# RWKV operands in one layout for both directions, elementwise steps on all 128 partitions of DVE, token shift read from the accumulators, Gram products in two halves of 64 columns

## The chip, the cores and the metric

The kernel runs on one core of a Trainium2 chip. The metric is the device time of one execution in microseconds, taken as the median of the runs. A core has a matrix engine (PE in the profile, with its weight loads apart as PEld), three engines for elementwise work (DVE, ACT and POOL), and SP, which here only issues DMAs. Each engine runs its own queue in order; semaphores tie the queues together.

## The reference

One block of a hybrid model: 512 latent tokens and 256 context tokens of width 1024 are normalised, modulated and projected by one wide matrix; three mixers (an RWKV-7 recurrence in both directions, a convolution of 31 taps, an mLSTM) work on the projections, are gated, merged and added to the input; an MLP follows. The change touches the RWKV features and their recurrence:

```python
def _token_shift(u, mu_prev, mu_next):
    prev = jnp.pad(u, ((0, 0), (1, 0), (0, 0)))[:, :-1]
    nxt = jnp.pad(u, ((0, 0), (0, 1), (0, 0)))[:, 1:]
    return u + mu_prev * (prev - u) + mu_next * (nxt - u)
...
    for d, (wd, ad) in enumerate(((wd_f, ad_f), (wd_b, ad_b))):
        w_log = -jax.nn.softplus(-(w0[d] + jnp.tanh(wd) @ w2[d]).astype(jnp.float32)) - 0.5
        decay = jnp.exp(-jnp.exp(w_log))
        a = jax.nn.sigmoid((a0[d] + ad @ a2[d]).astype(jnp.float32))
        k_d = k.astype(jnp.float32) * (1.0 + (a - 1.0) * k_a)
...
    def step(S, inp):
        w_t, k_t, v_t, kk_t, a_t = inp[:5]
        S = (S * w_t[:, :, None, :]
             - jnp.einsum('bhvk,bhk->bhv', S, kk_t)[..., None] * (kk_t * a_t)[:, :, None, :]
             + v_t[..., None] * k_t[:, :, None, :])
        y = jnp.einsum('bhvk,bhk->bhv', S, inp[5]) if emit else None
```

There are 8 heads of 64 channels, handled as 4 pairs. The recurrence runs over the context first and then over the latent tokens, forwards and backwards.

## The kernel before

Channels lie on partitions and tokens along the free axis. The matrices are fp32; a weight block of 128x512 is split into a rounded part (`whi`, cast on ACT, L152) and a remainder (`wlo`, subtracted on POOL, L153), and every product is three matmuls per block of 128 rows: x high by w high, x low by w high, x high by w low. `dense` (L250 and after) does this for one block of 128 outputs, into accumulators `dl` (512 latent tokens) and `dc` (256 context tokens) that share three PSUM buffers. It takes two such splits per call.

A scheduler that simulates the program puts the instructions of each engine in order; inside an engine that order is then fixed, so an instruction that waits holds up all that stand behind it on its engine. The program passes these stages, by the time of the trace: the norm and first modulation (0 to 54 us); the convolution's input and its first 62 taps (L291, on DVE), beside the shifted low-rank inputs and the keys (54 to 150); the receptances, the operands of the eight heads, the values and the rest of the convolution's input (150 to 322); the mLSTM with the other taps and the first pair's Gram products (322 to 597); the weaves (597 to 862), in which the chain of one pair, the gates' products and the next pair's preparation are interleaved; the last weave (862 to 1000); the merge and the MLP (1000 to 1430).

The *token shift* (`shifted`, L302) copies the accumulators to a padded tile `U` on ACT (L307, L311) and forms the three terms on DVE: `Ut` = om times `U` (L314), plus mu_p times `U` one token earlier (L315), plus mu_n times `U` one token later (L323).

The *operands* of head h (`operands`, L338) are made for both directions at once, forwards on partitions 0 to 63, backwards on 64 to 127. `BK` holds for each of 12 chunks of 64 tokens the normalised key kk and the key k, loaded from `kb` in the order kk, k on the first half and k, kk on the second. `ct` is the running sum of the log decay over a chunk (scans L365, L366, one for each direction on its half), `E` its Exp (L367, with a column of ones at each end of a chunk) and `en` the Exp of the opposite sign. `al` is kk times the shifted `E` (POOL, L379 and L380, on each half) and r times `E` (DVE, L382). `BK` is multiplied by `en` (POOL, four times L386), by 1 + the tanh of the learning rate on kk (DVE, L389, on each half) and by another function of it on k (DVE, L393, on each half). The results are spilled (`sp_al`, `sp_bk`) and loaded later.

The *Gram products* (`gram`, L973 and after) take, per head, direction and chunk, the 64 rows of that direction of `BK` as 128 stationary columns (both kinds) and of `AL` as streamed columns, 128 for a latent chunk and 64 for a context one (L989); DVE multiplies the results by the masks gmf and gmb into `LT`, `LR` and the other half of `AL` (L991 to L996). The *chain* (L1098) makes one step for both directions: `ch` = AL by SV (L1113), times the inverse `LT` (L1119), copied as U to `UV` (ACT, L1122), then the update of the state (L1128, L1129).

A table of the names in the rows: cy, cz, z and dwh belong to the taps; kb, BK, E, ct, cw, al, rd, PL to the operands; pg, AL, BK to the Gram products; dg (L531) are the gates' products.

## Time and profile before

| what | us |
| --- | --- |
| runs: 1431.49, 1431.73, 1427.99; median | 1431.49 |
| span of the profiled execution | 1429.6 |
| PE busy | 1271.3 (89%) |
| DVE busy | 903.0 (63%) |
| POOL busy | 689.4 (48%) |
| ACT busy | 496.4 (35%) |
| PE busy in 150 to 322 us | 128.4 of 172 |
| POOL busy in 150 to 322 us | 150.2 of 172 |
| DVE busy in 150 to 322 us | 146.9 of 172 |

Only the span is known of the profiled execution's own time; the median of the runs lies 1.9 us above it. A share of busy time over the whole span is a mean over stages with different limits, so the stages are read apart. An idle stretch has behind it, after an arrow, what ended it. Matmuls overlap, so that the busy time of a run of matmuls is less than the sum of their lengths; a logical fp32 product of the small kind is two passes in the trace.

### The profile page before, as it was taken

The numbers are of one execution on the slowest core, as the hardware profiler recorded it, in microseconds if no ns is written. First come the engines' busy times: TensorE is split into PE (matmuls) and PEld (weight loads), VectorE is DVE, ScalarE is ACT, GpSimd is POOL, SyncE is SP. The second block draws the span as 40 slices with busy tenths as digits, with TensorE's granted clock in tenths as the row PEclk, the third lists the DMA queues.
The fourth block names the chain that finished last, engine by engine and source line by source line (L and its number), as shares of the span: only waits on it lengthen the run. The fifth ranks groups of instructions, "written<-read, shape, count | busy, mean of one in ns | idle before, by whom it ended". The sixth has DMA issues, their size and how long they took to land.

```text
span 1429.6 us, 21049 instructions
## 1 busy us (share of the span) xinstructions
PE 1271.3 (89%) x7620; PEld 985.8 (69%) x7620; DVE 903.0 (63%) x1518; ACT 496.4 (35%) x1024; POOL 689.4 (48%) x651
## 2 busy tenths in 40 slices
PE   6989986857698989789989998888999999999997
PEld 1578765635587877566757665566778888888886
DVE  2689888988736699379598895868657543300202
ACT  3422534423222222134244344532354344422322
POOL 0463499990854544233243344533455454444442
PEclk9999998887899998899699998999999999999999
DMA  9211466554162232433244134587544433343332
GB/s 363 67 60 58 119 182 205 171 182 147 39 185 72 93 107 67 128 101 100 72 135 117 45 97 156 185 258 231 205 153 146 134 111 96 111 144 99 125 96 88
DMA packets 113359, 187.81 MB, mean 131 GB/s; under 512 B 23124, under 2 KB 41812, under 8 KB 112232
## 3 DMA queue, kind: packets, MB, share of 16 engines
q1 hardware_dynamic: 113256, 186.47, 41.6%
q8 instruction: 60, 0.98, 0.3%
q14 instruction: 43, 0.35, 0.1%
HBM read 148.64 MB, written 29.40 MB: 125 GB/s over the span
## 4 chain that ended last, share of the span: by engine, by line
PE 58%; DVE 21%; DMA 7%; POOL 7%; issue 5%; ACT 2%; SPq 1%; DVEq 0%; POOLq 0%; ACTq 0%
PE pt L1281 15%; PE pd L1350 12%; PE dl L262 8%; PE dg L531 5%; POOL wlo L153 4%; PE pg L989 3%; DMA wad<-wada 3%; DVE N L1032 3%; PE pr L215 2%; DVE tmp L1030 2%; PE dc L262 2%; DVE cy L291 2%; POOL BK L386 1%; PE ch L1113 1%; DVE N L1025 1%
## 5 line engine op out<-in xcount | busy, mean ns | idle before, releaser
L153 POOL TENSOR_TENSOR wlo<-raw,whi 128x512 fp32r<-128x512 f32 x296 | 440.3, 1493 | 492.9 <-ACT whi L152 437.6
L152 ACT CAST whi<-raw 128x512 fp32r<-128x512 f32 x296 | 181.8, 618 | 358.1 <-PE pt L1281 113.8
L262 PE MATMUL dl<-hh,wlo 128*128 128x512 f32 (+1 forms) x368 | 153.6, 418 | 24.8 <-POOL wlo L153 24.7
L262 PE MATMUL dl<-hh,whi 128*128 128x512 f32 (+1 forms) x368 | 154.5, 420 | 0.7 <-DVE lf L716 0.7
L262 PE MATMUL dl<-hl,whi 128*128 128x512 f32 (+1 forms) x368 | 152.6, 415 | 0.0
L1376 DVE TENSOR_TENSOR x<-pt,modb 128x512 f32<-128x512 f32 x8 | 5.5, 689 | 154.7 <-PE pt L1281 154.7
L1350 PE MATMUL pd<-h2l,whi 128*128 128x512 f32 (+1 forms) x272 | 102.6, 379 | 0.7 <-POOL h2l L1333 0.7
L262 PEld LDWEIGHTS dl<-hh,wlo 128*128 128x128 f32 (+1 forms) x368 | 73.6, 200 | 42.1 <-POOL wlo L153 26.6
L1350 PE MATMUL pd<-h2h,wlo 128*128 128x512 f32 (+1 forms) x272 | 102.0, 377 | 0.0
L1350 PE MATMUL pd<-h2h,whi 128*128 128x512 f32 (+1 forms) x272 | 101.1, 378 | 0.2 <-ACT h2h L1330 0.2
L1281 PE MATMUL pt<-whi,h1l 128*128 128x512 f32 x256 | 99.6, 389 | 0.0
L1281 PE MATMUL pt<-whi,h1h 128*128 128x512 f32 x256 | 99.6, 389 | 0.0
L1281 PE MATMUL pt<-wlo,h1h 128*128 128x512 f32 x256 | 99.1, 389 | 0.0
L262 PEld LDWEIGHTS dl<-hh,whi 128*128 128x128 f32 (+1 forms) x368 | 73.8, 200 | 17.0 <-DVE lf L716 2.1
L262 PEld LDWEIGHTS dl<-hl,whi 128*128 128x128 f32 (+1 forms) x368 | 73.6, 200 | 15.0 <-issue 0.5
L1126 POOL TENSOR_TENSOR sps<-SV,PL 64x128 f32<-64x128 f32 x88 | 40.1, 455 | 79.0 <-DVE SV L1129 75.5
L1354 DVE TENSOR_TENSOR relu<-relu 128x512 f32<-128x512 f32 x32 | 39.5, 1238 | 56.0 <-ACT relu L1353 55.9
L627 DVE SCALAR_TENSOR_TENSOR accm<-wad,sc,accm 128x512 f32<-128x512 f32 x56 | 56.7, 1013 | 27.0 <-DMA wad<-wada 26.6
L531 PE MATMUL dg<-hh,whi 128*128 128x512 f32 x144 | 66.5, 462 | 0.0
L531 PE MATMUL dg<-hl,whi 128*128 128x512 f32 x144 | 66.4, 461 | 0.0
L531 PE MATMUL dg<-hh,wlo 128*128 128x512 f32 x144 | 65.6, 456 | 0.0
L989 PE MATMUL pg<-AL,BK 64*128 64x128 f32 (+1 forms) x384 | 59.1, 311 | 5.5 <-DVE AL L996 4.5
(388 smaller groups left out, 2942.0 us busy)
## 6 DMA issues: line engine op xcount, KB each, us to landing
raw<-wblk SPq DMA_DIRECT2D x296, 256.0 KB, 2.8
wad<-wada SPq DMA_DIRECT2D x64, 256.0 KB, 3.8
wada<-wada SPq DMA_DIRECT2D x8, 1024.0 KB, 17.5
sp_bk<-BK SPq DMA_DIRECT2D x8, 768.0 KB, 3.5
BK<-sp_bk SPq DMA_DIRECT2D x8, 768.0 KB, 4.5
sp_g<-gt SPq DMA_DIRECT2D x24, 256.0 KB, 2.1
sp_al<-al SPq DMA_DIRECT2D x8, 640.0 KB, 3.2
AL<-sp_al SPq DMA_DIRECT2D x16, 256.0 KB, 5.8
```

The costliest lines, as they stand in the source:

```text
L152: A.copy(hi[:, :], raw[:, :])
L153: G.tensor_tensor(lo[:, :], raw[:, :], hi[:, :], ALU.subtract)
L215: PE.matmul(pr[:, :], lhsT=sc[:, k, :], rhs=wa[q * 2 + k // 4][:, k % 4, :], start=(k == 0), stop=(k == KT - 1))
L262: PE.matmul(ps_[0:M, :], lhsT=w[:, ko:ko + M], rhs=x[seg][:, k, :], start=(n == 0), stop=(n == 3 * KT - 1))
L531: yield lambda w=w, x=x, k=k, ko=ko, n=n: PE.matmul(ps[:, :], lhsT=w[:, ko:ko + P], rhs=x[:, k, :], start=(n == 0), stop=(n == 3 * KT - 1))
L627: V.scalar_tensor_tensor(o, t[:, :], sc[:, k, 0:1], o, ALU.mult, ALU.add)
L989: PE.matmul(ps[:, i, :, :], lhsT=BK[dd, c, :, :], rhs=AL[d][dd, b0:b0 + w, :], start=True, stop=True)
L1032: V.tensor_tensor(N[:, s + 1:32, 0:s], N[:, s + 1:32, 0:s], tv, ALU.add)
L1126: last["Pool"] = G.tensor_tensor(sps[hf], SV[d][hf, c, :, :], PL[hf, c, :].unsqueeze(2).to_broadcast([64, 2, CH]), ALU.mult)
L1281: PE.matmul(pss[i][:, :], lhsT=x[:, k, ts_], rhs=w[:, :], start=(k == 0 and n == 0), stop=(k == nk - 1 and n == 2))
L1350: PE.matmul(ps[:, ts_], lhsT=w[:, ko:ko + P], rhs=x[:, k, ts_], start=(k == 0 and n == 0), stop=(k == 7 and n == 2))
L1354: V.tensor_tensor(t[:, :], t[:, :], t[:, :], ALU.mult)
```

## The change

Five things, all on the RWKV path.

1. Token shift: `U` and `Ut` go. ACT writes om times the accumulator into the destination; two scalar_tensor_tensor of DVE per accumulator add the neighbours, read from PSUM at an offset of one (511 and 255 elements).
2. Operands: `BK` is loaded in the same order on both halves. `E` has no padding; a second tile `Ep` holds the shifted Exp, made by two more Exps on ACT, each on 64 partitions. The two products of `al` and the product of `BK` with `en` are one DVE operation each on 128 partitions, as are the two steps with the learning rate. POOL keeps the small copies to `PL`.
3. Keys: the shifted k goes to a tile of the "vj" tag; ACT writes it into `kb`, plain and scaled (before, DVE wrote both).
4. Gram products: 64 stationary columns at a time, kk's into the direction's own half of the PSUM partitions and k's into the other, so twice as many matmuls; `al` holds r first and then kk, and the masks' blocks are exchanged.
5. Chain: U of both directions lies on partitions 0 to 63, V on 64 to 127.

```diff
     def shifted(b, ctx, name, bufs=1, dst=None):
-        U = S1.tile([P, 771], F32, tag="U", name="U", bufs=2)
-        ps = dense(B_RW + b, True, ctx)
...
-        V.tensor_scalar(tmp[:, 0:n], U[:, 1:1 + n], om[:, b:b + 1], None, ALU.mult)
-        V.scalar_tensor_tensor(tmp[:, 0:n], U[:, 0:n], C("mu_p", b), tmp[:, 0:n], ALU.mult, ALU.add)
...
+        for ps, a, z in zip(pss, (0, NT), (NT, T)):
+            n = z - a
+            A.activation(dst[:, a:z], ps[:, :], AF.Copy, scale=om[:, b:b + 1])
+            V.scalar_tensor_tensor(dst[:, a + 1:z], ps[:, 0:n - 1], C("mu_p", b), dst[:, a + 1:z], ALU.mult, ALU.add)
+            V.scalar_tensor_tensor(dst[:, a:z - 1], ps[:, 1:n], C("mu_n", b), dst[:, a:z - 1], ALU.mult, ALU.add)
...
-        SY.dma_start(BK[HF[0]], kb[HF[h]])
-        for x in range(2):
-            SY.dma_start(BK[HF[1], :, x, :], kb[HF[h], :, 1 - x, :])
...
+            SY.dma_start(BK[HF[d]], kb[HF[h]])
...
-        A.activation(E[:, :, 1:CH + 1], ct.rearrange("p (c t) -> p c t", c=NCH), AF.Exp, scale=-0.5 * RALPHA)
+        A.activation(E[:, :], ctf, AF.Exp, scale=-0.5 * RALPHA)
+        A.activation(Ep[0:64, :, 1:CH], ct[0:64, :, 0:CH - 1], AF.Exp, scale=-0.5 * RALPHA)
+        A.activation(Ep[64:128, :, 0:CH - 1], ct[64:128, :, 1:CH], AF.Exp, scale=-0.5 * RALPHA)
...
-            G.tensor_tensor(ALl[:, :, 0, :], kk3[:, 0:8, :], E[dd, 0:8, o:o + CH], ALU.mult)
-            G.tensor_tensor(al[dd, 16:20, :], kk3[:, 8:12, :], E[dd, 8:12, o:o + CH], ALU.mult)
...
+        V.tensor_tensor(al[:, 8 * CH:20 * CH].rearrange("p (c t) -> p c t", t=CH), BK[:, :, 0, :], Ep[:, :, :], ALU.mult)
+        V.tensor_tensor(al[:, 0:8 * CH], rj[:, :], E[:, 0:NT], ALU.mult)
...
-                G.tensor_tensor(BK[:, c, x, :], en3[:, c, :], BK[:, c, x, :], ALU.mult)
...
-            V.scalar_tensor_tensor(BK[dd, :, d, :], ta3[dd], 1.0, BK[dd, :, d, :], ALU.add, ALU.mult)
...
+        V.tensor_tensor(BK[:, :, :, :], BK[:, :, :, :], en3.unsqueeze(2).to_broadcast([P, NCH, 2, CH]), ALU.mult)
+        V.scalar_tensor_tensor(BK[:, :, 0, :], ta3, 1.0, BK[:, :, 0, :], ALU.add, ALU.mult)
...
+        V.tensor_tensor(BK[:, :, 1, :], ta3, BK[:, :, 1, :], ALU.mult)
...
+        kj = shifted(4 + j, True, "vj", 2).rearrange("p (c t) -> p c t", t=CH)
+        A.copy(kb[:, :, 1, :], kj)
+        A.activation(kb[:, :, 0, :], kj, AF.Copy, scale=C("kk", j))
...
-                    PE.matmul(ps[:, i, :, :], lhsT=BK[dd, c, :, :], rhs=AL[d][dd, b0:b0 + w, :], start=True, stop=True)
...
+                    for x, hf in ((0, dd), (1, od)):
+                        PE.matmul(ps[hf, i, :, :], lhsT=BK[dd, c, x, :], rhs=al[:, c] if lat else AL[d][dd, 8 + c:9 + c, :],
+                                  start=True, stop=True)
...
-                    last["PE"] = PE.matmul(ch[hf, 1, h, :], lhsT=TT[hf, h * 12 + c, :], rhs=xs[hf, h, :], start=True, stop=True)
+                    last["PE"] = PE.matmul(ch[HF[0], 1, h, :], lhsT=TT[hf, h * 12 + c, :], rhs=xs[hf, h, :], start=True, stop=True)
...
-                last["ACT"] = A.copy(UV[d][hf, c, :, :], ch[hf, 1])
+                last["ACT"] = A.copy(UV[d][HF[0], c, :, :], ch[HF[0], 1])
```

The scheduler then writes another order. On DVE, at the first token shift among the taps, before:

```order
L291 SCALAR_TENSOR_TENSOR cy_564<-z_563,dwh,cy_564 128x512
L291 SCALAR_TENSOR_TENSOR cy_483<-z_482,dwh,cy_483 128x512
L291 SCALAR_TENSOR_TENSOR cy_564<-z_563,dwh,cy_564 128x512
L291 SCALAR_TENSOR_TENSOR cy_483<-z_482,dwh,cy_483 128x512
L291 SCALAR_TENSOR_TENSOR cy_564<-z_563,dwh,cy_564 128x512
L314 TENSOR_SCALAR Ut<-U,dv 128x769
L291 SCALAR_TENSOR_TENSOR cy_483<-z_482,dwh,cy_483 128x512
L291 SCALAR_TENSOR_TENSOR cy_564<-z_563,dwh,cy_564 128x512
L315 SCALAR_TENSOR_TENSOR Ut<-U,par,Ut 128x769
```

and the same place now, from the same tap on (the lines of the changed kernel have other numbers: the taps are still L291, L310 and L311 are the two neighbours of the token shift, `dl` and `dc` the accumulators):

```order
L291 SCALAR_TENSOR_TENSOR cy_564<-z_563,dwh,cy_564 128x512
L310 SCALAR_TENSOR_TENSOR vj<-dl,par,vj 128x511
L291 SCALAR_TENSOR_TENSOR cy_483<-z_482,dwh,cy_483 128x512
L291 SCALAR_TENSOR_TENSOR cy_564<-z_563,dwh,cy_564 128x512
L311 SCALAR_TENSOR_TENSOR vj<-dl,par,vj 128x511
L291 SCALAR_TENSOR_TENSOR cy_483<-z_482,dwh,cy_483 128x512
L310 SCALAR_TENSOR_TENSOR vj<-dc,par,vj 128x255
L291 SCALAR_TENSOR_TENSOR cy_564<-z_563,dwh,cy_564 128x512
```

The first operation of the token shift moved four taps forward, and it is one that reads an accumulator.

On DVE, in the middle of the operands, one head before (with pieces of its neighbours, which is how the order mixes them):

```order
L365 SCALAR_TENSOR_TENSOR ct<-scm,cw 64x768
L366 SCALAR_TENSOR_TENSOR ct<-scm,cw 64x768
L389 SCALAR_TENSOR_TENSOR BK<-ct,BK 64x12x64
L382 TENSOR_TENSOR al<-rd,E_715 128x8x64
L389 SCALAR_TENSOR_TENSOR BK<-ct,BK 64x12x64
L281 SCALAR_TENSOR_TENSOR U<-tg,dl 128x8x64
L393 TENSOR_TENSOR BK<-ct,BK 64x12x64 x2
L365 SCALAR_TENSOR_TENSOR ct<-scm,cw 64x768
```

and one head now (L352 and L353 are the scans, L366 and L367 the products of `al`, L370 the product with `en`, L371 and L373 the steps with the learning rate):

```order
L352 SCALAR_TENSOR_TENSOR ct<-scm,cw 64x768
L353 SCALAR_TENSOR_TENSOR ct<-scm,cw 64x768
L367 TENSOR_TENSOR al<-rd,E_716 128x512
L366 TENSOR_TENSOR al<-BK,Ep_717 128x768
L370 TENSOR_TENSOR BK<-BK,cw 128x1536
L371 SCALAR_TENSOR_TENSOR BK<-ct,BK 128x12x64
L281 SCALAR_TENSOR_TENSOR U<-tg,dl 128x8x64
L373 TENSOR_TENSOR BK<-ct,BK 128x12x64
L352 SCALAR_TENSOR_TENSOR ct<-scm,cw 64x768
```

What POOL did between has come to DVE, and the next head's scans stand behind the last product of this one. On POOL, the same place before:

```order
L153 TENSOR_TENSOR wlo<-raw,whi 128x512
L386 TENSOR_TENSOR BK<-cw,BK 128x6x64 x2
L379 TENSOR_TENSOR al<-BK,E_715 64x8x64
L380 TENSOR_TENSOR al<-BK,E_715 64x256
L279 MEMSET U 128x8x15
L280 MEMSET U 128x8x15
L386 TENSOR_TENSOR BK<-cw,BK 128x6x64 x2
L379 TENSOR_TENSOR al<-BK,E_715 64x8x64
L380 TENSOR_TENSOR al<-BK,E_715 64x256
L153 TENSOR_TENSOR wlo<-raw,whi 128x512
```

and now (L363 are the copies to `PL`):

```order
L363 COPY PL<-E_714 64x12 x2
L153 TENSOR_TENSOR wlo<-raw,whi 128x512 x9
L363 COPY PL<-E_716 64x12 x2
L153 TENSOR_TENSOR wlo<-raw,whi 128x512 x7
L363 COPY PL<-E_714 64x12 x2
```

Between two heads' copies only the splits of the weights are left on POOL.

## Rows read from the trace of the kernel before

**Rows 1.** Stages: start:end, length, busy us (x instructions) per engine, PEclk, DMA share, GB/s
```profile
54.00:150.00 96.00, 90.03 (x469) 76.42 (x467) 79.69 (x101) 27.20 (x52) 52.52 (x63) 0.95 0.23 69
150.00:322.00 172.00, 128.36 (x567) 97.66 (x566) 146.86 (x118) 70.88 (x117) 150.15 (x133) 0.88 0.60 175
...
597.00:862.00 265.00, 247.68 (x2426) 178.73 (x2427) 207.12 (x404) 100.58 (x283) 92.37 (x127) 0.91 0.34 100
```

**Rows 2.** Groups, 150 to 322 us: xcount | busy us, mean ns | idle before, releasers
```profile
L386 POOL TENSOR_TENSOR BK<-cw,BK 128x384 f32<-128x384 f32 x32 | 52.7, 1660 | 0.5
L153 POOL TENSOR_TENSOR wlo<-raw,whi 128x512 fp32r<-128x512 f32 x27 | 46.5, 1728 | 7.3 <-ACT whi L152 6.4 <-PE dl L262 0.6
...
L389 DVE SCALAR_TENSOR_TENSOR BK<-ct,BK 64x768 f32<-64x768 f32 x16 | 30.0, 1874 | 13.3 <-POOL BK L386 13.1
L379 POOL TENSOR_TENSOR al<-BK,E 64x512 f32<-64x512 f32 x16 | 26.2, 1635 | 4.3 <-DMA BK<-kb 3.5
L393 DVE TENSOR_TENSOR BK<-ct,BK 64x768 f32<-64x768 f32 x16 | 24.6, 1540 | 4.0 <-ACT ct L390 3.7
L366 DVE TENSOR_TENSOR_SCAN ct<-scm,cw 64x768 f32<-64x768 bf16 x8 | 19.4, 2423 | 0.1
...
L365 DVE TENSOR_TENSOR_SCAN ct<-scm,cw 64x768 f32<-64x768 bf16 x8 | 16.6, 2073 | 4.3 <-ACT cw L363 4.3
L380 POOL TENSOR_TENSOR al<-BK,E 64x256 f32<-64x256 f32 x16 | 16.3, 1016 | 0.0
...
L382 DVE TENSOR_TENSOR al<-rd,E 128x512 f32<-128x512 f32 x8 | 10.7, 1343 | 0.1
...
L381 POOL COPY PL<-E 64x12 f32<-64x12 f32 x16 | 9.2, 575 | 7.1 <-ACT E L367 6.7
...
L367 ACT ACTIVATE E<-ct 128x768 f32<-128x768 f32 x8 | 6.8, 846 | 49.5 <-DVE ct L366 49.5
```

**Rows 3.** Single lines, whole run: ns min/median/max, first and last start us, shapes
```profile
L153 POOL TENSOR_TENSOR wlo<-raw,whi x296: 1253/1289/18832, 32.4 to 1408.7; 128x512 fp32r<-128x512 f32 x148
...
L389 DVE SCALAR_TENSOR_TENSOR BK<-ct,BK x16: 952/1914/3808, 182.8 to 314.1; 64x768 f32<-64x768 f32 x16
...
L366 DVE TENSOR_TENSOR_SCAN ct<-scm,cw x8: 1753/2406/2691, 154.1 to 294.3; 64x768 f32<-64x768 bf16 x8
...
L382 DVE TENSOR_TENSOR al<-rd,E x8: 682/1502/1743, 156.9 to 298.9; 128x512 f32<-128x512 f32 x8
...
L441 DVE TENSOR_TENSOR bo<-hs,vj x4: 675/692/692, 276.3 to 325.6; 128x512 f32<-128x512 f32 x4
```

**Rows 4.** Timeline of POOL, DVE and PE about 83 to 100 us: start, length, instructions, idle
```profile
85.14 14.81 POOL L153 TENSOR_TENSOR wlo<-raw,whi 128x512 fp32r<-128x512 f32 x1 [5.14 <-ACT whi L152]
...
82.97 8.03 DVE L291 SCALAR_TENSOR_TENSOR cy<-z,dwh,cy 128x512 f32<-128x512 f32 x12
...
100.00 0.80 PE L262 MATMUL dl<-hh,wlo 128*128 128x512 f32 x1 [5.27 <-POOL wlo L153]
```

**Rows 5.** The same about 365 to 386 us, during the later taps
```profile
366.80 20.07 POOL L153 TENSOR_TENSOR wlo<-raw,whi 128x512 fp32r<-128x512 f32 x2 [3.90 <-ACT whi L152]
...
365.22 19.29 DVE L291 SCALAR_TENSOR_TENSOR cy<-cz,dwh,cy 128x512 f32<-128x512 f32 x29
...
385.69 0.80 PE L262 MATMUL dl<-hh,wlo 128*128 128x512 f32 x1 [13.27 <-POOL wlo L153]
```

**Rows 6.** Timeline of PE, four runs of small products (two of latent, context Grams)
```profile
498.20 1.16 PE L989 MATMUL pg<-AL,BK 64*128 64x128 f32 x8
...
614.87 1.17 PE L989 MATMUL pg<-AL,BK 64*128 64x64 f32 x12
...
746.23 0.47 PE L1128 MATMUL ch<-UV,BKt 128*64 128x64 f32 x8
746.63 1.10 PE L989 MATMUL pg<-AL,BK 64*128 64x64 f32 x8
```

**Rows 7.** Chain of waits of 597 to 862 us, its shares by line
```profile
by line: PE dg L531 23.3%; PE pg L989 14.1%; DVE N L1032 8.8%; DVE tmp L1030 6.9%; issue 4.9%; DVE N L1025 4.7%; PE ch L1113 4.3%; PE ch L1119 4.2%; PE pbk L1011 3.1%; PE ch L1128 3.1%; DVE SV L1129 2.5%; DVE LT L1055 2.2%; PE py L1094 2.2%
```

More of the change, by code (lines that the diff above doesn't have):

```diff
@@ L332, in build @@
     G.memset(mk[64:128, :, CH - 1:CH], 0.0)
-    Es = [SO.tile([P, NCH, CH + 2], F32, name=f"E{i}") for i in range(2)]
-    for E in Es:
-        G.memset(E[:, :, 0:1], 1.0)
-        G.memset(E[:, :, CH + 1:CH + 2], 1.0)
+    Es = [(SO.tile([P, T], F32, name=f"E{i}"), SO.tile([P, NCH, CH], F32, name=f"Ep{i}")) for i in range(2)]
+    for _, Ep in Es:
+        G.memset(Ep[0:64, :, 0:1], 1.0)
+        G.memset(Ep[64:128, :, CH - 1:CH], 1.0)
     def operands(j, h, kb, r):
@@ L368, in operands @@
         en = cw
-        A.activation(en[:, :], ct[:, :], AF.Exp, scale=0.5 * RALPHA, bias=epsc[:, 4:5])
-        ta = ct
+        A.activation(en[:, :], ctf, AF.Exp, scale=0.5 * RALPHA, bias=epsc[:, 4:5])
+        ta = ctf[:, :]
         low_rank(ta, 1, adt, a0h)
-        r3 = rj.rearrange("p (c t) -> p c t", c=8)
-        ta3, en3 = (t.rearrange("p (c t) -> p c t", c=NCH) for t in (ta, en))
-        al = SO.tile([P, 20, CH], F32, tag="al", name="al", bufs=2)
+        E3 = E.rearrange("p (c t) -> p c t", t=CH)
@@ L383, in operands @@
-        SY.dma_start(sp["al", hd][:, :], al.rearrange("p c t -> p (c t)"))
-        for x in range(2):
-            for c in (slice(0, 6), slice(6, 12)):
-                G.tensor_tensor(BK[:, c, x, :], en3[:, c, :], BK[:, c, x, :], ALU.mult)
-        for d in range(2):
-            dd = HF[d]
-            V.scalar_tensor_tensor(BK[dd, :, d, :], ta3[dd], 1.0, BK[dd, :, d, :], ALU.add, ALU.mult)
-        A.activation(ta[:, :], ta[:, :], AF.Identity, scale=ka5[:, hd:hd + 1], bias=oka[:, hd:hd + 1])
@@ L391, in operands @@
-        for d in range(2):
-            dd = HF[d]
-            V.tensor_tensor(BK[dd, :, 1 - d, :], ta3[dd], BK[dd, :, 1 - d, :], ALU.mult)
+            G.tensor_copy(PL[HF[d], j, :, h:h + 1], E3[HF[d], :, CH - 1:CH] if d == 0 else E3[HF[d], :, 0:1])
+        al = SO.tile([P, 20 * CH], F32, tag="al", name="al", bufs=2)
+        V.tensor_tensor(al[:, 8 * CH:20 * CH].rearrange("p (c t) -> p c t", t=CH), BK[:, :, 0, :], Ep[:, :, :], ALU.mult)
+        V.tensor_tensor(al[:, 0:8 * CH], rj[:, :], E[:, 0:NT], ALU.mult)
@@ L1110, in chain @@
             for d, c, ch, hf in zip(range(2), cs, chs, HF):
-                a_ = 2 * c if c < 8 else 8 + c
+                a_ = 8 + c
                 for h in range(2):
@@ L1131, in chain @@
                 if c < 8:
-                    last["ACT"] = A.copy(self.UU[hf, c, :, :], ch[hf, 1])
+                    last["ACT"] = A.copy(self.UU[hf, c, :, :], ch[HF[0], 1])
             yield last
@@ L1474, in layout @@
     lt, le = (i[:, None] < i[None]).astype(f), (i[:, None] <= i[None]).astype(f)
-    gmf = np.block([[-lt, le], [lt, le]])
-    gmb = np.block([[lt.T, le.T], [-lt.T, le.T]])
+    gmf = np.block([[le, -lt], [le, lt]])
+    gmb = np.block([[le.T, lt.T], [le.T, -lt.T]])
     bones = np.kron(np.eye(2), np.ones((64, 64))).astype(f)
```

64 lines of the change are left out of this document (24 added, 40 removed).

## The prediction, made before the changed kernel ran

> **What bounds the kernel now.** I read the table of stages first, with PE's busy time and granted clock beside the other engines, because a mean over the whole span hides that the limits change. The weaves late in the program are TensorE's: PE is busy 247.7 of 265 us there [rows 1]. The stretch from 150 to 322 us is not. There PE is busy 128 of 172 us at a granted clock of 0.88, while POOL is busy 150 and DVE 147 [rows 1]. PE's own work there, at the full clock, is about 128.4 x 0.88 = 113 us. So 59 us of this stretch are lost to someone else.
>
> The groups of that stretch say to whom [rows 2]. POOL's 150 us are the split of the weights (wlo, 27 of them, 46.5 us), which every dense product of PE needs, and in the same in-order queue the elementwise work of `operands`: L386 52.7, L379 26.2, L380 16.3 and the copies L381 9.2 us. DVE's part of `operands` is L389 30.0, L393 24.6 and the scans L366 19.4 and L365 16.6 us.
>
> Third, the spread of the durations [rows 3]. Operations of DVE that read two SBUF operands stretch: L389 takes 0.95 us at best, 1.91 in the middle, 3.81 at worst, the scan 1.75 to 2.69, L382 0.68 to 1.74. L441, which reads one operand from a PSUM accumulator, stays at 0.68 to 0.69 in all four. And wlo goes from 1.29 (median of the whole run) to a mean of 1.73 in this stretch [rows 2, 3]. DVE and POOL take turns here; their 147 and 150 us are largely each other's waiting.
>
> The same is seen plainly in two places outside. During a run of 12 taps on DVE, one wlo lies 14.81 us in POOL, and PE waits 5.27 us for it [rows 4]; during a run of 29 taps two wlo take 20.07 us and PE waits 13.27 [rows 5].
>
> **The change part by part.** The sum is made against the profiled execution's 1429.6 us; the median of the runs, 1431.5, is 1.9 us above it, added at the end.
>
> *Operands.* POOL loses L386, L379 and L380: 52.7 + 26.2 + 16.3 = 95.2 us of the 150. It keeps wlo, 27 x 1.29 = 35 us when nothing stands in its way, and the copies, 9 us: 44 us. DVE gets the whole elementwise work, one operation on 128 partitions where there were two on 64. An operation's time goes by the elements of a partition: L389 does 768 in 0.95 us at best on 64 partitions, L382 does 512 in 0.68 on 128 [rows 3]. I take 0.95 for each of the three 128x768 operations (kk times the shifted Exp, the scalar_tensor_tensor, the last product), 0.68 for r times E, two scans of 1.75, and for the 128x1536 product, which the trace does not have, twice 0.95 as its dearer end (the cheaper: 1.5, by the slope of 0.27 us for 256 elements between 512 and 768). Per head 3.5 + 0.7 + 3 x 0.95 + 1.9 = 8.9 us, for eight heads 71; the order shows the scans of the first head among the taps of the stage before, so 68 here. DVE's other work in the stretch is now 146.9 - (30.0 + 24.6 + 19.4 + 16.6 + 10.7 for L382) = 46 us (L382: eight times its mean 1.34). Between 30 (unstretched, and the token shift with fewer elements) and 46 remain, so DVE needs 98 to 114.
>
> What may overlap decides. If POOL's 44 us had to go wholly between DVE's operations the stretch would be 98 + 44 = 142. If all of it goes beside operations that read an accumulator and beside DVE's own waits, PE's 113 is the floor. I count two thirds of the 44 as hidden, since the token shift, the bonus, the gates and the normalisation now feed DVE from PSUM: 98 + 15 = 113 to 114 + 15 = 129. I take 127, near the upper end, as queues run in order and PE still waits here and there: **-45 us** (bounds -59 and -30). ACT gets two more Exps per head, each on half the partitions, 2 x 0.85 x 8 = 14 us by the Exp L367 [rows 2]; with 71 of 172 us now [rows 1] it would be at 85 of 127, so I cost it at nothing, and rival 4 takes that cover away. The swapped loads of BK become plain ones of the same bytes; L379 waited 3.5 us in all for them [rows 2], so zero.
>
> *Token shift.* Ut and U go; ACT writes the scaled middle term and DVE adds two terms per accumulator, read from PSUM. Each costs 0.69 for 512 elements by L441 [rows 3]; four of them (511, 511, 255, 255) cost what the three operations did within half a microsecond, so the count gives no term, and the scale of kb moved to ACT is hidden under PE there. What moves is the order: the first such operation stands four taps earlier than Ut did. The run of 12 that kept POOL out from 85.1 us on [rows 4] has a PSUM reader after its eighth tap, at about 83.0 + 8 x 0.67 = 88.3 us. If POOL gets in there, wlo is done near 90 instead of 99.95, and PE's 5.27 us go. What is late next is PE itself (90 of 96 us busy [rows 1]), so no more than that plus a little clock: **-5 us** (bounds -10 and 0: POOL may need a longer opening than one operation of 0.7 us). The cost: an accumulator is held until DVE has read it four times; three exist, so a late DVE now holds PE directly, where ACT's copy freed it before. Nobody but PE waits for that; it is in rival 4.
>
> *Taps later.* In the new order some 18 taps of the second half are done earlier, and the run after the gate rows has 25 instead of 29: 4 x 0.67 = **-3 us** of the 13.27 us wait [rows 5]; bounds -13 (if POOL gets in) and 0.
>
> *Gram products.* A group was 8 passes through a 64x128 tile, 1.16 us with 128 columns streamed and 1.10 with 64 [rows 6]: the streamed columns hardly count, the 128 columns of the stationary operand do. Now there are 16 passes through 64x64 tiles, alternating between the two column halves. L1128 does 8 passes, four in each column half, in 0.47 us [rows 6], so 16 of that kind are 0.94. For the 16 context groups (64 streamed) I take -0.25 each, -4 us; for the 32 latent ones (128 streamed) zero, between -0.2 and +1.16 each. **-4 us** together (bounds -10 and +37, rival 1).
>
> *Chain.* Both directions' U now land on partitions 0 to 63, so the two directions of L1119 keep different row halves but share the columns. Row halves that share columns do run side by side: 12 passes of the Gram products, two directions, took 1.17 us, as long as 8 of one [rows 6]. Zero; at worst the four passes of one direction come behind those of the other, half of an L1128 row's 0.47 us in 48 steps, +11.
>
> Sum: -45 - 5 - 3 - 4 = -57; 1429.6 - 57 = 1372.6, and with 1.9 us **1374 us**.
>
> **The rivals.** *1. The two column halves don't overlap.* Then each of the 16 passes costs what one costs now, 0.145 us: +1.16 x 32 + 1.10 x 16 = +55 us of PE. The Gram products hold 14.1% of the chain of the weaves, 37 of 265 us [rows 7], of 48 x 1.15 = 55 in all, so two thirds count: +37, **1411 us**. For it: the halves read the same rows. Against it: L1128 [rows 6]. The Trainium skill, "TensorE: Matmul & The Clock Gate", Part 3 on packing small matmuls, speaks for it: a weight load overlaps matmuls in flight only when its row group differs, and here it is the same. By that rule the sum is this rival's; L1128's row, whose halves also share all rows, disagrees.
>
> *2. DVE starves POOL (slower than before).* POOL's wlo must now get past bursts of two-operand work on DVE that are all on one engine. As in [rows 4, 5], a wlo could lie until the burst ends. There are 13 dense blocks (27 wlo, two each) in the stretch; if each waits through one head's 8.9 us, PE needs 113 + 13 x 8.9 = 229 us, 57 more than now; with the other terms' -12 on the median that is 1431.5 + 45 = **1476 us**. It decides from (172 - 113) / 13 = 4.5 us of wait per block. For it: 14.81 and 20.07 us, both measured. Against it: a head's operations wait for ACT's Exps between them, which leaves openings that the independent taps don't have, and weights are prepared ahead.
>
> *3. Everything opens.* The stretch falls to PE's 113 (-59), POOL gets in during the later taps too (-13), the first taps give their whole -10, the Gram products -4: 1431.5 - 86 = **1346 us**, rounded. For it: L441's steady time. Against it: DVE alone needs 98 to 114.
>
> *4. The bound goes to the chain of one head.* Scans 3.5, four Exps in a row on ACT 3.4, the 1536 product 1.9, two of 0.95, ACT's scaling of ta between them about an Exp's 0.85, and hand-overs: some 12 to 15 us a head, and in the new order the next head's scans stand behind the last product of the one before. With DVE's other 30 us not fitting into the gaps, 8 x 15 + 30 = 150 us: -22 instead of -45, **1397 us**; with accumulators held by a late DVE up to no gain at all, 1431. For it: ACT's Exps already wait 49.5 us for the scans [rows 2]. Against it: the other 30 us are mostly independent of the head in hand.
>
> **How the numbers follow.** My forecast 1374: 0.60. Rival 1: 0.10. Rival 2: 0.08. Rival 3: 0.10. Rival 4: 0.12, of which two thirds faster, 0.03 the same, 0.01 slower. The forecast's own bounds are 1429.6 + 1.9 - 57 with -14 to +15 from the operands and a few us from the rest, 1355 to 1394. To leave out no more than 0.2 the range reaches to rival 1 above and to rival 3 below: 1344 to 1411. This kernel's runs tell a change from none from about 0.3%, 4 us. Faster by more: 0.60 + 0.10 + 0.10 + 0.08 = 0.88; the same 0.03; slower 0.08 + 0.01 = 0.09.
>
> **What would show it.** In the stretch that ends with the gate rows: POOL down from 150 to 45 to 65 us, PE's clock above 0.88, the length near 127; L389's successors near 0.95, the 1536 product between 1.5 and 1.9. In the taps: no wlo of 14.81 us. On PE: a latent Gram group still near 1.16 us (2.3 shows rival 1), the context group below 1.1, the chain's L1119 still 0.46 for eight passes. Wrong would be: PE idle for wlo behind DVE in the operands (rival 2), or DVE idle for ACT's Exps with PE waiting for accumulators (rival 4).

## The result and the profile after

The changed kernel takes 1373.6 us (median of four runs, 1366.4 to 1377.4) against 1430.8 of the kernel before, timed beside it: the ratio is 0.9596, 95% interval 0.9556 to 0.9635. In a later series it was 1368.0 us, ratio 0.957 (0.9546 to 0.9593).

Its profiled execution has a span of 1375.3 us, 54.3 less. The same instructions in both traces show where these went (each time is the start of the instruction named, of before and of after):

| from the start, us | before | after | difference | of the stage |
| --- | --- | --- | --- | --- |
| first block product of the first receptance | 155.2 | 155.5 | +0.3 | +0.3 |
| last bonus product (hs) | 322.8 | 273.6 | -49.2 | -49.5 |
| first product of the chain (ch) | 596.1 | 541.9 | -54.2 | -5.0 |
| last product of the chain | 940.1 | 883.8 | -56.3 | -2.1 |
| end of the span | 1429.6 | 1375.3 | -54.3 | +2.0 |

So nine tenths of the gain are there by the last bonus product. Not all of it is time saved in that stretch. PE makes 408 passes of dense blocks (`dl` and `dc`) between these two marks before and 360 after; the other 48 now stand behind the second mark, in a stage that is 5 us shorter all the same. At dense blocks with the same number of passes done, the changed kernel is ahead by 38.5 us (286.1 against 324.6) and, one block on, by 49.8 (298.4 against 348.2). The windows between these marks say how it looks now; the columns are those of [rows 1] (start:end, length, busy us of PE, PEld, DVE, ACT, POOL with their instructions, PEclk, DMA share, GB/s). Before:

```profile
155.00:323.00 168.00, 124.16 (x546) 94.01 (x544) 142.07 (x114) 69.52 (x114) 149.53 (x130) 0.88 0.60 176
323.00:596.00 273.00, 228.11 (x1364) 189.82 (x1362) 195.86 (x453) 68.88 (x123) 124.45 (x112) 0.89 0.32 100
```

After:

```profile
155.00:274.00 119.00, 105.41 (x492) 81.19 (x491) 97.83 (x104) 74.46 (x116) 49.16 (x41) 0.95 0.81 240
274.00:542.00 268.00, 226.97 (x1508) 189.26 (x1507) 192.65 (x453) 69.55 (x125) 128.15 (x114) 0.93 0.34 104
```

In the first row POOL has gone from 150 to 49 us and DVE, although it does POOL's work now, from 142 to 98. PE is busy 105 of 119 us at a clock of 0.95 (0.88 before), so its own work there, at the full clock, is 105.4 x 0.95 = 100 us. The second row is nearly as before; PE's 144 instructions more are the halved Gram products (96) and the 48 dense passes.

The groups of the changed kernel from 150 to 273 us, which answer to [rows 2] (xcount, then busy us, mean ns, idle time before):

```profile
L153 POOL TENSOR_TENSOR wlo<-raw,whi 128x512 fp32r<-128x512 f32 x24 | 45.2, 1890 | 58.7 <-ACT whi L152 42.6 <-DMA raw<-wblk 6.5 <-PE dl L262 4.9
...
L370 DVE TENSOR_TENSOR BK<-BK,cw 128x1536 f32<-128x1536 f32 x8 | 15.1, 1892 | 0.5
...
L371 DVE SCALAR_TENSOR_TENSOR BK<-ct,BK 128x768 f32<-128x768 f32 x8 | 10.6, 1323 | 0.3
...
L373 DVE TENSOR_TENSOR BK<-ct,BK 128x768 f32<-128x768 f32 x8 | 8.8, 1094 | 4.4 <-ACT ct L372 4.4
L366 DVE TENSOR_TENSOR al<-BK,Ep 128x768 f32<-128x768 f32 x8 | 8.3, 1035 | 4.8 <-DMA BK<-kb 4.2 <-ACT Ep L356 0.2
...
L354 ACT ACTIVATE E<-ct 128x768 f32<-128x768 f32 x7 | 5.9, 846 | 9.3 <-DVE ct L353 9.3
L355 ACT ACTIVATE Ep<-ct 64x756 f32<-64x756 f32 x7 | 5.9, 837 | 6.1 <-DVE ct L352 6.1
...
L367 DVE TENSOR_TENSOR al<-rd,E 128x512 f32<-128x512 f32 x8 | 5.5, 693 | 1.9 <-ACT E L354 1.8
...
L363 POOL COPY PL<-E 64x12 f32<-64x12 f32 x14 | 4.8, 341 | 13.3 <-ACT E L354 12.9
```

POOL now waits for ACT's casts of the weights (42.6 us): it has become the one that waits. ACT waits 9.3 us for the scans, where it waited 49.5 [rows 2].

### The profile page after: what moved, and what is told of

Its sections match the earlier page's. It is cut to its first block, busy times and chain, and to the rows that moved or that the text cites. A ratio compares the mean times of both kernels' runs of the same rounds, so it can differ in the third digit from the quotient of the medians.

```text
span 1375.3 us, 21700 instructions
## 1 busy us (share of the span) xinstructions
PE 1252.9 (91%) x8004; PEld 969.6 (71%) x8004; DVE 849.2 (62%) x1509; ACT 511.8 (37%) x1048; POOL 585.7 (43%) x547
## 4 chain that ended last, share of the span: by engine, by line
PE 45%; DVE 14%; DMA 5%; issue 3%; ACT 1%; POOL 1%; SPq 0%; DVEq 0%; POOLq 0%; ACTq 0%
PE pt L1268 16%; PE pd L1337 13%; PE dg L512 5%; DMA wad<-wada 4%; DVE N L1019 3%; DVE tmp L1017 2%; PE pg L973 2%; PE ch L1100 1%; PE pd L682 1%; DVE N L1012 1%; PE ch L1106 1%; DVE accm L608 1%; PE dl L262 1%; PE pbk L998 1%; PE ch L1115 1%
## 5 line engine op out<-in xcount | busy, mean ns | idle before, releaser
L153 POOL TENSOR_TENSOR wlo<-raw,whi 128x512 fp32r<-128x512 f32 x296 | 435.5, 1477 | 555.5 <-ACT whi L152 488.9
L262 PE MATMUL dl<-hh,wlo 128*128 128x512 f32 (+1 forms) x368 | 149.7, 407 | 10.8 <-POOL wlo L153 10.8
L262 PE MATMUL dl<-hh,whi 128*128 128x512 f32 (+1 forms) x368 | 151.4, 412 | 2.7 <-ACT kT L758 1.9
L262 PE MATMUL dl<-hl,whi 128*128 128x512 f32 (+1 forms) x368 | 148.5, 403 | 0.0
L262 PEld LDWEIGHTS dl<-hh,wlo 128*128 128x128 f32 (+1 forms) x368 | 70.7, 192 | 26.0 <-POOL wlo L153 11.2
L262 PEld LDWEIGHTS dl<-hl,whi 128*128 128x128 f32 (+1 forms) x368 | 70.8, 192 | 15.2 <-issue 1.5
L1019 DVE TENSOR_TENSOR N<-N,tmp 128x30 f32<-128x30 f32 (+14 forms) x120 | 58.1, 484 | 3.0
```

The lines of the kernel that those rows point to most:

```text
L153: G.tensor_tensor(lo[:, :], raw[:, :], hi[:, :], ALU.subtract)
L262: PE.matmul(ps_[0:M, :], lhsT=w[:, ko:ko + M], rhs=x[seg][:, k, :], start=(n == 0), stop=(n == 3 * KT - 1))
L1019: V.tensor_tensor(N[:, s + 1:32, 0:s], N[:, s + 1:32, 0:s], tv, ALU.add)
```

## The experiments

Each kernel is one edit of the kernel before or of the changed one. A ratio is to the kernel before, timed on the same chip, with its 95% interval. Beside the whole time I read two things from each trace: the length of the stretch from the first receptance's first block product to the last bonus product, and the start of the first product of the chain. Both are steadier than the whole: two profiles of the changed kernel agree within 1.6 us on the place of each block product up to 506 us and within 0.8 us on the chain's first product, and differ by 8 us at the end.

The stretch has a weakness. The scheduler orders every kernel anew, so that other dense passes lie in it each time. The first product of the chain has all dense passes before it in every kernel (1104 of `dl`, 456 of `dc`) and prices an edit better, up to there; what becomes of it by the end is a question of its own:

| kernel | stretch, us | dense passes in it | first product of the chain, us | ahead of before, us |
| --- | --- | --- | --- | --- |
| before | 167.6 | 408 | 596.1 | |
| changed | 118.1 | 360 | 541.9 | 54.2 |
| token shift alone (in before) | 136.4 | 360 | 561.2 | 34.9 |
| operands alone (old token shift in changed) | 145.3 | 456 | 560.6 | 35.5 |
| neighbours from SBUF (in changed) | 133.8 | 401 | 548.3 | 47.8 |
| product with en on DVE (in before) | 165.0 | 430 | 589.2 | 6.9 |
| product with en on POOL (in changed) | 126.3 | 360 | 549.0 | 47.1 |
| hs in another buffer (in before) | 134.5 | 336 | 589.6 | 6.5 |
| hs in another buffer (in changed) | 97.7 | 336 | 537.5 | 58.6 |

### The parts alone

The Gram products alone, in the kernel before:

```diff
-                    PE.matmul(ps[:, i, :, :], lhsT=BK[dd, c, :, :], rhs=AL[d][dd, b0:b0 + w, :], start=True, stop=True)
+                    for x in range(2):
+                        PE.matmul(ps[HF[x], i, :, :], lhsT=BK[dd, c, x, :], rhs=AL[d][dd, b0:b0 + w, :], start=True, stop=True)
```

> The kernel before with one edit: each Gram matmul of 128 stationary columns is two of 64, one for each kind of column; layout and results as before. If the column halves overlap (my theory): a latent group of 16 passes stays at 1.1 to 1.2 us (8 passes took 1.16 before), a context group falls from 1.10 to about 0.7, as in the trace of the changed kernel (1.09 and 0.68); PE is busy some 9 us less, of which the end sees 0 to 6: 1425 to 1431 us. If they don't overlap: 2.0 to 2.3 us a group, +25 to +37 us: 1455 to 1468 us.

Measured: ratio 0.9988 (0.9948 to 1.0028), no difference. Its latent groups take 1.09 us; the timeline of PE (start, length, instructions):

```profile
483.60 1.09 PE L990 MATMUL pg<-AL,BK 64*64 64x128 f32 x16
```

The halves overlap, and the end gains nothing that the spread of the runs would show (they go from 1413 to 1432 us; in the profiled one the chain takes 331 us from its first to its last product, 344 before, more than the Gram products could give). The same rows of the changed kernel, a latent and a context group and one step of the chain:

```profile
427.90 1.09 PE L973 MATMUL pg<-AL,BK 64*64 64x128 f32 x16
```

```profile
373.55 0.68 PE L973 MATMUL pg<-AL,BK 64*64 64x64 f32 x16
```

```profile
572.60 0.45 PE L1106 MATMUL ch<-xc,LT 64*64 64x64 f32 x8
```

Sixteen passes of 64 columns take 1.09 where eight of 128 took 1.16, and 0.68 where they took 1.10 [rows 6]; the chain's eight passes with shared columns take 0.45.

The token shift alone, in the kernel before (with the keys' copies on ACT, as in the change):

```diff
-        U = S1.tile([P, 771], F32, tag="U", name="U", bufs=2)
...
+            A.activation(dst[:, a:z], ps[:, :], AF.Copy, scale=om[:, b:b + 1])
+            V.scalar_tensor_tensor(dst[:, a + 1:z], ps[:, 0:n - 1], C("mu_p", b), dst[:, a + 1:z], ALU.mult, ALU.add)
+            V.scalar_tensor_tensor(dst[:, a:z - 1], ps[:, 1:n], C("mu_n", b), dst[:, a:z - 1], ALU.mult, ALU.add)
```

> The kernel before with the new token shift and the keys' copies on ACT alone. Theory A: the wait of PE for one wlo during the first taps (5.27 us) is on the path; with an operation that reads an accumulator earlier among the taps the wlo of 14.81 us falls to about 6 us and the end comes 5 us earlier: 1424 to 1427 us. Theory B: it is given back within the same stage, because the accumulators are now held until DVE has read them four times and DVE is full there: the wlo falls all the same, PE gets new waits for DVE's reads, and the end moves by less than 3 us: 1428 to 1434 us.

Measured: 1395.2 us, ratio 0.9805 (0.9753 to 0.9857). Neither theory: both looked at the taps alone, where theory B was right (the first receptance begins at 157.0 us), and the part is worth 28 us (0.0195 x 1430; 20 to 35 by the interval). Its stretch is 136.4 us, 31 less than before with 48 dense passes fewer in it, and the first product of the chain comes 34.9 us earlier.

The operands (with the Gram products and the chain) alone: the changed kernel with the old token shift.

```diff
+        tmp = S1.tile([P, 769], F32, tag="Ut", name="Ut", bufs=1)
+        V.tensor_scalar(tmp[:, 0:n], U[:, 1:1 + n], om[:, b:b + 1], None, ALU.mult)
...
-        lor = SO.tile([P, 2, P], F32, tag="lor", name="lor", bufs=2)
+        lor = SO.tile([P, 2, P], F32, tag="lor", name="lor", bufs=1)
```

> The changed kernel with the old token shift put back (padded copy U, three terms on DVE from SBUF; one buffer each for Ut and for the low-rank weights, since two don't fit beside the new tiles). The token shift alone took 28 us off the kernel before. Theory P (prediction: the operands' rearrangement carries the gain and the token shift is worth little beside it): 1375 to 1385 us. Theory S (the two parts add: token shift 28, operands the remaining 21 to 28 us): 1398 to 1412 us, with PE waiting again for the values (tp) behind DVE.

Measured: 1396.3 us, ratio 0.9779 (0.973 to 0.9827), 32 us (25 to 39); the stretch is 145.3 us, 22 less than before with 48 dense passes more in it, and the first product of the chain comes 35.5 us earlier. In the whole the two parts add within their intervals: 28 + 32 = 60, 57 and 61 together. At the first product of the chain they overlap: 34.9 + 35.5 = 70.4, 54.2 together, so that each is worth 19 us there when the other is already in. Theory S is nearer than theory P, but 1396.3 lies below its span, and the wait that it named did not come back: PE waits 2.0 us for the values behind DVE's bo, against 21.6 before. This kernel also has a cost of its own: PE waits 4.1 us in all for the low-rank weights, which have a single buffer here. The windows of the two, in the same columns as above; the token shift alone:

```profile
157.00:293.00 136.00, 110.48 (x488) 84.45 (x487) 105.72 (x94) 61.93 (x102) 122.38 (x94) 0.89 0.70 193
```

The operands alone:

```profile
156.00:301.00 145.00, 128.25 (x592) 99.45 (x591) 124.92 (x129) 86.60 (x135) 58.16 (x67) 0.94 0.71 215
```

Without the operands' edit POOL is busy 122 of 136 us, without the token shift's DVE 125 of 145. Each part leaves the other engine nearly full.

### Why the token shift is worth so much

The changed kernel, with the neighbours read from a copy in SBUF; the same operations of DVE, and the accumulator freed early:

```diff
             A.activation(dst[:, a:z], ps[:, :], AF.Copy, scale=om[:, b:b + 1])
-            V.scalar_tensor_tensor(dst[:, a + 1:z], ps[:, 0:n - 1], C("mu_p", b), dst[:, a + 1:z], ALU.mult, ALU.add)
+            A.copy(U[:, 0:n], ps[:, :])
+            V.scalar_tensor_tensor(dst[:, a + 1:z], U[:, 0:n - 1], C("mu_p", b), dst[:, a + 1:z], ALU.mult, ALU.add)
```

> The changed kernel with the two neighbour terms of the token shift read from a copy in SBUF (one more ACT copy per accumulator, which frees the accumulator as before) in place of the accumulator; the same number of DVE operations. The token shift gives 23 us on top of the other changes (1396 to 1374). Theory T (what counts is that DVE's operations then read one SBUF operand and don't take turns with POOL): most of it is lost, 1384 to 1396 us, with wlo longer in the taps. Rival O (fewer and shorter operations, no U and Ut, another order): 1370 to 1378 us. Rival H (the held accumulators cost more than the reads from PSUM save): 1366 to 1371 us.

Measured: 1387.9 us, ratio 0.9714 (0.9683 to 0.9745), 14 to 20 us slower than the changed kernel's two medians. The token shift gives 23 to 28 us on top of the rest, so in the whole theory T looks like two thirds of it. The trace gives it less. The first product of the chain starts at 548.3 us, 6.4 later than in the changed kernel; with the old token shift it is 18.7 later. That is a third. DVE's busy time in the terms of all token shifts says the same: 46.5 us with the old one (and 2.5 for the scaled keys), 38.3 with the copy in SBUF, 31.9 in the changed kernel. So the source of the operand counts (theory T), and so do the fewer and shorter operations (rival O). The stretch is 15.7 us longer, but it holds 41 dense passes and the scans of one head more. What makes up the rest of the 14 to 20 us, behind the chain's first product, is not shown. The scheduler's order is another here, too, and ACT makes one more copy (it is busy 86 of 134 us); neither was tested by itself.

That the source counts is plain from the terms themselves (ns least/median/most, first and last start). In the changed kernel, from the accumulator, and then from the copy in SBUF:

```profile
L310 DVE SCALAR_TENSOR_TENSOR vj<-dl,par,vj x11: 733/746/750, 87.7 to 270.7; 128x511 f32<-128x511 f32 x11
```

```profile
L312 DVE SCALAR_TENSOR_TENSOR vj<-U,par,vj x21: 465/750/1769, 89.6 to 280.4; 128x511 f32<-128x511 f32 x11, 128x255 f32<-128x255 f32 x10
```

In the taps, POOL's splits (timeline of POOL; start, length, instructions, idle before) show it as well. With the copy in SBUF:

```profile
97.64 13.47 POOL L153 TENSOR_TENSOR wlo<-raw,whi 128x512 fp32r<-128x512 f32 x4 [9.89 <-ACT whi L152]
```

The first of these four takes 8.41 us by itself, beside taps and terms that read two SBUF operands, and ends at about 106, after a copy of DVE that reads one:

```profile
103.06 1.40 DVE L291 SCALAR_TENSOR_TENSOR cy<-z,dwh,cy 128x512 f32<-128x512 f32 x2
104.39 0.54 DVE L381 COPY adt<-vj 128x768 f32<-128x768 f32 x1
```

In the changed kernel, where the one of 14.81 us stood before [rows 4], the first of two takes 4.36 us and ends at 89.0, after the first term that reads the accumulator (at 87.7):

```profile
84.61 6.06 POOL L153 TENSOR_TENSOR wlo<-raw,whi 128x512 fp32r<-128x512 f32 x2 [5.14 <-ACT whi L152]
```

### Turns, or POOL's queue?

One step moved in either direction. From the kernel before, the product with en to DVE:

```diff
-        for x in range(2):
-            for c in (slice(0, 6), slice(6, 12)):
-                G.tensor_tensor(BK[:, c, x, :], en3[:, c, :], BK[:, c, x, :], ALU.mult)
+        V.tensor_tensor(BK[:, :, :, :], BK[:, :, :, :], en3.unsqueeze(2).to_broadcast([P, NCH, 2, CH]), ALU.mult)
```

> The kernel before with one step moved: the product of BK with en as one 128x1536 operation of DVE a head, not four on POOL. Theory T (turns): POOL loses 32 x 0.99 = 32 us unstretched, DVE gets 8 x 1.89 = 15, the stretch of 172 us falls by about 17 to 155, the whole to 1411 to 1418 us. Theory Q (POOL's queue alone was the bound): POOL's 150 us fall by its busy 52.7, the stretch to 120 to 125 us, the whole to 1379 to 1384 us.

Measured: 1419.5 us, ratio 0.9938 (0.9909 to 0.9967), 9 us (5 to 13) faster. And from the changed kernel the same step back to POOL, as the lines with a minus above:

> The changed kernel with one step put back: the product of BK with en on POOL as four operations of 128x384 a head, not one of 128x1536 on DVE. Theory T (DVE's operations with two SBUF operands and POOL's take turns, so that their unstretched times add): POOL gets 32 x 0.99 = 32 us, DVE loses 8 x 1.89 = 15; the stretch of the operands grows from 123 to about 140 us, the whole to 1388 to 1394 us. Theory Q (only the length of POOL's own queue counted): POOL's 51 us grow to about 85 to 105, still under the stretch's 123, so no change: 1371 to 1377 us.

Measured: 1386.7 us, ratio 0.9709 (0.9683 to 0.9735), 13 to 19 us slower than the changed kernel; its stretch is 126.3 us, 8.2 longer. Theory Q is out on both sides: 53 us of POOL's busy time taken away gave 9, and 31 us added to a POOL that was idle for more than half of the stretch cost 13 to 19. Theory T has the sign but is too large in the stretch: 17 us said, 2.6 and 8.2 found (165.0 against 167.6 us, 126.3 against 118.1). By the first product of the chain both come to 7 us, 6.9 earlier and 7.1 later. The window of the first shows what a sum of turns leaves out:

```profile
157.00:322.00 165.00, 130.11 (x566) 98.49 (x565) 149.71 (x135) 73.97 (x118) 100.82 (x98) 0.90 0.64 187
```

POOL fell from 150 to 101 us and DVE rose to 150 of 165: one moved step passes most of the load to DVE.

### Waits that looked like the bound

PE waited 21.6 us before for DVE's bo, at the single buffer of the value transposes. The kernel before with hs in another buffer:

```diff
-        pl = PS1.tile([P, NT], F32, tag="tp", name="hs", bufs=1)
+        pl = PS1.tile([P, NT], F32, tag="n", name="hs", bufs=2)
```

> The kernel before with one edit: the bonus product hs takes a buffer of the tag n (two, used by the normalisation before) in place of the one tp buffer of the value transposes. PE waited 21.6 us at tp for DVE's bo between 155 and 348 us. Theory W (this in-order wait of PE through the single buffer is what the stretch loses): the wait goes and the end comes 12 to 22 us earlier, 1405 to 1418 us. Theory T (DVE and POOL bound the stretch and PE would wait elsewhere): less than 5 us, 1422 to 1430 us, with PE waiting for wlo or for the operands in place of tp.

Measured: ratio 0.9996 (0.9961 to 1.0031), nothing. PE's waits for the transposes' buffer (tp) from 155 to 348 us, before (who waits, for what, us in total, times, longest):

```profile
PE tp L434 <- DVE bo L441: 21.6, 3, 13.6
PE tp L434 <- DVE vj L323: 6.0, 1, 6.0
```

and with the edit, in a profile of 1443.7 us:

```profile
PE tp L434 <- DVE vj L323: 23.3, 4, 8.2
```

Of 27.6 us, 23.3 are left, all under the other name: PE waited for DVE, whichever of its operations came last. This kernel also shows what the stretch is worth as a measure: its last bonus product comes 33 us sooner after the first receptance (134.5 us against 167.6), with 72 dense passes put off behind it, and the whole is the same. Nor is the first product of the chain the end: it comes 6.5 us sooner here, and the whole shows nothing of that. The same edit in the changed kernel:

> The changed kernel with the same edit (hs in the tag n). PE waits 7.4 us at hs for ACT's copy vt through the single buffer there. Theory W: these go, 1366 to 1370 us. Theory T (DVE or ACT are full in that stretch all the same): 1371 to 1377 us.

Measured: 1367.1 us, ratio 0.9573 (0.9516 to 0.963); beside the changed kernel's 0.9596 and 0.957 it is not told apart.

The one long wait for POOL that the change left is in the later taps. POOL, DVE and PE of the changed kernel, which answer to [rows 5]:

```profile
326.56 16.70 POOL L153 TENSOR_TENSOR wlo<-raw,whi 128x512 fp32r<-128x512 f32 x1 [3.64 <-ACT whi L152]
```

```profile
325.49 16.65 DVE L291 SCALAR_TENSOR_TENSOR cy<-cz,dwh,cy 128x512 f32<-128x512 f32 x25
```

```profile
343.32 0.80 PE L262 MATMUL dl<-hh,wlo 128*128 128x512 f32 x1 [10.81 <-POOL wlo L153]
```

The split lies in POOL as long as the taps run. The changed kernel with the remainders of four blocks on DVE:

```diff
-        G.tensor_tensor(lo[:, :], raw[:, :], hi[:, :], ALU.subtract)
+        (V if b in ONDVE else G).tensor_tensor(lo[:, :], raw[:, :], hi[:, :], ALU.subtract)
...
+    ONDVE = (B_ML + 0, B_ML + 12, B_ML + 5, B_ML + 9)
```

> The changed kernel with the remainder wlo of four weight blocks of the first two mLSTM heads made on DVE, not POOL (eight instructions of 128x512, which stand among the later taps in DVE's order). In the changed kernel one of them lies 16.7 us in POOL behind 25 taps and PE waits 10.8 us. Theory T (POOL is kept out by runs of two-operand work on DVE): the wait goes, 1361 to 1367 us. Rival (the mLSTM's chain behind it is later anyway, or the eight instructions delay the gate rows on DVE by as much): 1370 to 1377 us.

Measured: 1365.9 us, ratio 0.9577 (0.9517 to 0.9638). The wait for wlo is gone, each of the eight subtractions takes 0.67 us on DVE, and the first product of the chain starts at 531.6 us, 10.3 earlier than in the changed kernel. In the whole it can't be told apart from the changed kernel's two medians, since the time from the first product of the chain to the last is 348.6 us here and 342 and 336 in the changed kernel's two profiles. Both edits together, and the changed kernel beside them on the same chip:

> The changed kernel with hs in the tag n and with the remainders of four mLSTM blocks on DVE. If the two waits that they take away (7.4 and 10.8 us of PE in the profile of the changed kernel) are both on the path: 1355 to 1361 us. If only the wait for wlo is: 1361 to 1367 us. If neither is beyond the spread of the runs: 1368 to 1378 us.

> The changed kernel itself again, on the same chip as the next one, as its measure: 1368 to 1378 us.

Measured: 1365.6 us (ratio 0.9561, 0.9538 to 0.9584) and 1368.0 us (0.957, 0.9546 to 0.9593). 1365.6 is where it should be if only the wait for wlo counted, but the changed kernel itself came out 5 us lower than in its first series, and the 2.4 us between the two lie within the intervals. The first product of the chain starts at 536.3 us against 541.1. It may be a little better; the runs don't show that it is.

### Why the first taps gave nothing

The last question is why the 5.4 us that PE is ahead of before at the second token shift are gone at the first receptance (155.5 against 155.2 us). In the kernel below ten taps of each of the first two tiles are left out.

```diff
-        for k in range(31):
+        for k in range(n):
...
-    taps(tiles)
+    taps(tiles, 21)
```

> The changed kernel with 21 of the 31 taps of the first two convolution tiles (ten left out on each: 20 operations of DVE, 13.4 us). The question is why the 5.4 us that PE was ahead in the first taps are given back before the first receptance, whose dense block begins at 155.5 us in the changed kernel, 155.2 before, 155.4 with the neighbours read from SBUF. If DVE is full there (taps, token shift and the first head's scans): that block begins 4 to 9 us earlier, at 147 to 152 us. If PE's own work sets it: less than 1 us.

Measured: that block begins at 149.1 us, 6.4 earlier, and PE is 6.1 us ahead of before there (one run, 1382 us, tells nothing on the whole). By the first product of the chain 2.3 us of the 6.4 are left (539.6 against 541.9). Its window, and that of the changed kernel from 53 us on, show DVE's share:

```profile
54.00:150.00 96.00, 93.89 (x495) 80.53 (x495) 65.74 (x88) 40.00 (x66) 40.01 (x47) 0.98 0.25 82
```

```profile
53.00:150.00 97.00, 92.09 (x470) 78.11 (x471) 79.15 (x102) 42.06 (x71) 45.34 (x46) 0.96 0.23 72
```

With less on DVE, PE is at its own 94 of 96 us. In the changed kernel DVE is full from 104.6 to 126.2 us (21.5 of 21.6 us busy), among other things with the first head's scans, which stood behind this stage before, and PE waits for the accumulator that DVE is still to read:

```profile
114.93 0.39 PE L262 MATMUL dc<-hh,whi 128*128 128x256 f32 x1 [3.42 <-DVE vj L311]
```

## Why the prediction was right, and where its parts were not

The total, 1374 us, is what was measured in the first series (1368 in the later one), and the direction and the place (the stretch of operands, -45 predicted and -49.5 measured) were read from the right row: POOL and DVE both busy for most of 172 us [rows 1] and their operations stretched [rows 3]. That it came out to the microsecond is luck: the division among the parts was wrong, and their errors cancel. The parts of the sum stand as follows.

*Operands, -45.* The stretch lost 49.5 us, but the prediction wrote this down to the operands, and the operands alone (with the Gram products and the chain) are worth 32 us of the whole and 35.5 at the first product of the chain; with the token shift already in, 19.3 there. The prices of the operations were good: the 1536 product 1.76 us in the middle and 1.89 in the mean (1.9 taken), the others 0.95 at best, as taken, and 0.96 to 1.21 in the middle:

```profile
L370 DVE TENSOR_TENSOR BK<-BK,cw x8: 1746/1759/2849, 171.5 to 265.0; 128x1536 f32<-128x1536 f32 x8
```

```profile
L371 DVE SCALAR_TENSOR_TENSOR BK<-ct,BK x8: 946/1206/1833, 176.0 to 266.9; 128x768 f32<-128x768 f32 x8
```

```profile
L373 DVE TENSOR_TENSOR BK<-ct,BK x8: 953/958/2049, 178.6 to 269.8; 128x768 f32<-128x768 f32 x8
```

(ns least/median/most, first and last start.) DVE needed 98 us of the stretch, the lower end of the 98 to 114 that the prediction bounded, and POOL 49.

*Token shift, -5.* This is the step that failed, and twice. "The count gives no term" priced four operations against three by their length when undisturbed, equal within half a microsecond. Measured, DVE was busy 51.6 us with the old terms of fifteen token shifts and 31.9 us with the new ones, and it lost the scaling of the keys, 2.5 us. By the least time of each shape the old terms come to 38 us: half a microsecond in each of fifteen is some 6 us, and the other 13 were stretch, in the receptances and values as well as in the taps (L323 took 0.47 to 1.51 us for 256 elements). The new ones did not stretch. On top of the other changes this is worth 18.7 us at the first product of the chain and 23 to 28 in the whole. Of that the operand's source is a third by the trace (6.4 us in e3_sbuf) and two thirds by the whole times; the share stays open. The prediction had the observation (L441 never stretches [rows 3]) and used it to hide POOL's 44 us and to bring DVE's other work down to 30, but gave the token shift no line of its own, so the gain was put down to the operands. And the 5 us that it did write down came (the split of 14.81 us is gone) and were given back in the same stage, because DVE is full there (21.5 of 21.6 us busy; e12_taps21), not PE, which the prediction named as next. The error of +5 there and of -4.5 in the stretch cancel in the total.

*Later taps, -3.* This is right in its place. The wait of PE at the taps' run fell from 13.27 to 10.81 us, as four taps fewer say, and the lead over the kernel before grows by 3.0 us across it (from 42.7 to 45.7). The stage around it lost 5.0 us in all: the lead falls from 49.2 to 42.7 at the gate rows, where the order is another, and grows again by 8.5 between the taps' run and the chain. These two were not pursued.

*Gram products, -4.* A group is shorter by 0.07 us (latent; zero taken) and by 0.42 (context; 0.25 taken). The streamed columns, which the prediction held to count hardly at all, do count in the small tiles: 1.09 with 128, 0.68 with 64. On the end nothing of it is to be seen: the chain's stretch went by 2.1 us, and e1_gram gave 0.9988 with an interval that holds 1. Mis-sized by not asking what share of it the path sees. The chain's zero held: 0.45 us for eight passes, 0.46 before.

*Rivals.* Rival 1 (no overlap of column halves) is out, 1.09 us against 2.3. The Trainium skill, "TensorE: Matmul & The Clock Gate", Part 3 on packing small matmuls, says that a weight load overlaps matmuls in flight only when its row group differs; here all sixteen loads are of the same row group, and the sixteen passes are shorter than the eight before. The trace disagrees, as L1128's row did. Rival 2 (DVE starves POOL): the splits in the stretch grew to a mean of 1.89 us, from 1.73 [rows 2], and PE never waited there for one, so the gaps were enough. Which of DVE's gaps POOL used was not looked at. Rival 3's two openings: the first came most of the way (from 150 us on, 123 us against a floor of 113), the second did not (10.81 us of wait are left). Rival 4 did not come: DVE waited some 6 us in all for ACT's Exps and scaling (the idle times of L373, L367 and L366 above).

A rule that the prediction did not use points at the missing term: the Trainium skill, "SBUF — State Buffer", "Who interferes with whom", has it that a DVE instruction with two SBUF inputs contends with a GpSimd instruction that reads SBUF, and one with at most one SBUF input, outside the 2-port perf modes, doesn't. The runs agree: the terms with one SBUF input take 0.75 us at most (L310), the same terms with two up to 1.77 (e3_sbuf, L312). The count of operands alone is not the whole of it, though. L314, the old scaling, read one SBUF operand, and it took from 0.61 to 1.65 us for the same 769 elements.

## What to carry to other kernels

Where DVE and POOL are both busy for most of a stretch, price every operation of DVE by what it takes there, not by its length when undisturbed, and list its SBUF operands: the same terms took up to 1.77 us from SBUF and 0.75 at most from an accumulator. The token shift's edit was worth nearly as much here (28 us) as moving 95 us of work off POOL (32), part by the source and part by shorter operations. Price a step in every stage in which it occurs, also where the change is not aimed. A mark inside the program prices an edit only where the same work lies before it: one edit brought the last bonus product 33 us nearer and the end not at all. A long wait for an engine that is full is not removed by giving the waiter another buffer; most of the wait only changes its name.
